# Gradient of a weight by Strassen pairs: one more pair, G's sums in one addition, PSUM banks filled ahead by ScalarE

## The chip, the cores and the metric

The kernel runs on one core of a Trainium2 chip. The metric is the device time of one execution in microseconds; a median over several runs is given. A core has a matrix engine (TensorE, in the profile PE for matmuls and PEld for loads of the stationary operand), a vector engine (VectorE, DVE), a scalar engine (ScalarE, ACT), GpSimd (POOL), which here only issues loads, and SyncE (SP), which issues stores. TensorE reads from SBUF and accumulates into PSUM; DVE and ACT move results from PSUM to SBUF.

## What is computed

```python
batch, m, k, n = 16, 512, 1024, 768
# input X: (16, 512, 1024) f32, grad_output G: (16, 512, 768) f32
grad_weight = np.einsum('bmk,bmn->kn', input, grad_output)   # (1024, 768) f32
```

With the batch and the rows taken together this is one product: the transpose of X (8192 x 1024) times G (8192 x 768), a sum over 8192 rows.

## The kernel before

The 8192 rows are taken in 32 units of 256 rows, two row tiles of 128 each. GpSimd's DMAs load a unit of X and of G and turn it from f32 to bf16 on the way. The output is cut into four quarters by X's columns (two halves of 512) and G's columns (two halves of 384): A and B are the left and right quarter of the upper half, C and D of the lower half. A quarter is four blocks of 128 x 384, one for each q, and each block takes one PSUM bank.

A unit is one of two kinds, by a letter of LOADS. For an "s" unit each of its two row tiles is multiplied plainly into A, B, C and D: 4 x 4 matmuls a tile, 32 a unit. A "P" unit is one step of Strassen's method on the 2 x 2 blocks that its two row tiles form: seven products in place of eight, each of four matmuls, 28 a unit, for the price of sums and differences of blocks that DVE makes first. Two of the seven products go to A and D directly; the other five (m, n, o, p, q) are gathered in `macc` and added to two quarters each at the end ("shares").

```python
LOADS = "sssssssPPPPPPPPPPPPPPPPPPPPPPPss"        # 9 single units, 23 pairs
...
def sum_g1(i):                                       # sums for pair i
    ge = sums.tile([P, 3, NH], bf16, name="ge")
    xe = sums.tile([P, 3, KH], bf16, name="xe")
    g = gp.rearrange("p m (h n) -> p m h n", h=2)
    nc.vector.tensor_add(out=ge[:, 0:2, :], in0=g[:, :, 0, :], in1=g[:, :, 1, :])     # L131
def sum_g2(i):
    nc.vector.tensor_add(out=extra[i][1][:, 2, :], in0=gp[:, 0, 0:NH], in1=gp[:, 1, NH:N])  # L135
def sum_g3(i):
    g = gp.rearrange("p m (h n) -> p (m h) n", h=2)
    nc.vector.tensor_sub(out=g[:, 1:3, :], in0=g[:, 1:3, :], in1=g[:, 3::-3, :])     # L140
def sum_x1(i): ...   # 1024 elements, L145
def sum_x2(i): ...   # 512 elements, L149
def sum_x3(i): ...   # 1024 elements, in place, L154
```

The order of all work is fixed by hand in a list of visits. `B14:2!0,2,0,0` means: visit product B, with its tiles up to the fourteenth; ACT takes the last two of its four banks and DVE the others; the exclamation mark closes the visit's banks, and the four numbers tell how many pieces of DVE work (sums for later pairs, shares) are put ahead of the drain of each bank. A number in front of the letter tells how many are put ahead of the visit. A visit that isn't closed stays open, and a later visit of the same product goes on in its banks. The eight banks form two slots of four, so two products are open at most.

```python
slots = [0, 1]
...
        if opening:
            slot = slots.pop(0)
            for q in range(Q):
                bank = psum.tile([P, 512], f32, name=f"bank{slot * Q + q}")[:, 0:NH]
                act = q >= Q - byact
                carried = act and not fresh[p]
                if carried:
                    nc.scalar.copy(out=bank, in_=sum_of(p, q))      # L266: ACT fills the bank with the sum so far
        ...
        nc.tensor.matmul(bank, stat, mov, start=..., stop=...)     # L285
        ...
        def shut(q):
            fill(ahead[q])
            if act:
                nc.scalar.copy(out=dst, in_=bank)                   # L299: ACT drains
            elif fresh[p]:
                nc.vector.tensor_copy(out=dst, in_=bank)            # L301
            else:
                nc.vector.tensor_add(out=dst, in0=bank, in1=dst)    # L303: DVE drains and adds
            if final and p in "ABCD":
                nc.sync.dma_start(out=OUT[...], in_=dst)
```

So a bank of ACT is first filled with the sum so far, which the matmuls then add to, and copied back at the end; a bank of DVE is added to the sum at the end. The last bank of the last visit is split into 256 and 128 columns (L336), with an addition and a store for each (L344). The very first tiles come as f32 over the queues of SP and ACT and are cast by DVE and ACT (`round_by`, L206), so that TensorE can start before GpSimd's first load lands; twelve matmuls of ones (L89) come before them.

Of the kernel before, what the change touches and what calls it, by code (L numbers as in the profile page):

```python
# [8 lines left out]

P = 128  # L10

LOADS = "sssssssPPPPPPPPPPPPPPPPPPPPPPPss"

ORDER = (
    "A1:3!0,0,0,0 D1:1 C2:4!0,0,0,0 B2:2!0,0,0,0 D3!0,0,0,0 A2 B4:1!0,0,0,0 A3 C4:2!0,0,0,0 "
    "A4!0,0,0,0 D5 D6!0,0,0,0 C6 B5 B6 B7 B8 C8!0,0,0,0 A8:1!0,0,0,0 D10:2!0,0,0,0 B10!0,0,0,0 "
    "A10:4 A12!0,0,0,0 C11!0,0,0,0 B14:2!0,2,0,0 C14:1!0,0,0,0 2D14:2 2A15:2!3,0,0,1 o2:4!2,0,0,0 "
    "m2:4!0,3,0,0 D15 n2:2!0,0,1,0 D16!0,0,0,0 q3:4!0,1,0,2 A16 p1:3 2p4!2,1,1,0 A18!2,0,0,0 m4:2 "  # L20
    "o5:4!2,2,0,0 m5!0,0,1,0 D19:1 4q6:4!2,0,0,0 D20!1,0,0,0 p5 p6 o7:1!1,0,0,0 n5:1 n7!5,0,0,0 "
    "p8 A20:4 3A22!3,0,1,0 p9!1,0,0,1 m9:3 D23:4!0,2,2,1 q10!1,0,1,0 m10 4o10:4 m11!0,1,0,0 "
    "o11!1,0,0,0 1n10 n11 2n12!2,0,0,0 p12:3!0,0,0,0 1A23 A24 1A25 1o13:3!3,0,0,2 A27!0,0,0,0 "
    "q12:3 D27:4 2q14!5,0,1,1 D28 1m15:2!2,0,0,2 p16:1!0,2,0,0 1D30!0,0,0,2 A30!0,0,0,0 o17:3 q16 "
    "8q18!0,0,0,1 o18 n16:4 4n19!0,2,0,3 D32 o20!1,0,1,1 D33 q20:2!1,0,0,0 D34!1,0,0,2 1m20:2 "
    "p17:4 m21!4,0,0,0 1p20 p22 3q22:2 3p23!2,0,0,0 q23!0,0,0,0 o23!0,0,0,0 A34:0-q m23:4!4,1,0,0 "
    "A37 n23:4!0,3,1,0 A41!1,0,1,0 C15:0+p C18!0,1,0,0 B18:4!0,0,1,2 D41!4,0,1,0 "
).split()


SHARES = (
    "t20 t21 t22 t23 t10 t11 t12 t13 l10 l11 l12 l13 l20 l21 l22 l23 l30 l31 l32 l33 "
).split()

WARMUP = [512] * 10 + [128] * 2
# [7 lines left out]
def kernel(  # L43
# [6 lines left out]
    nc = tc.nc  # L50
# [7 lines left out]
    NH = N // 2  # L58
    Q = KH // P

    X = input.rearrange("b m k -> (b m) k")
    G = grad_output.rearrange("b m n -> (b m) n")
    OUT = out.rearrange("(ks p) n -> p ks n", p=P)
# [14 lines left out]

    xf = [pairs.tile([P, K], f32, name=f"xf{s}", tag="xp") for s in range(2)]
    gf = pairs.tile([P, N], f32, name="gf", tag="gp")  # L80
    nc.sync.dma_start(out=gf[:, 0:NH], in_=G[0:P, 0:NH])  # L81
    nc.scalar.dma_start(out=xf[0], in_=X[0:P, :])
    nc.sync.dma_start(out=gf[:, NH:N], in_=G[0:P, NH:N])
    nc.scalar.dma_start(out=xf[1], in_=X[P : 2 * P, :])

    ones = nc.const_aps.tensor(1.0, (P, P), bf16)
# [38 lines left out]
    def sum_g1(i):  # L125
        _, xp, gp = items[i]
        ge = sums.tile([P, 3, NH], bf16, name="ge")
        xe = sums.tile([P, 3, KH], bf16, name="xe")
        extra[i] = (xe, ge)
        g = gp.rearrange("p m (h n) -> p m h n", h=2)  # L130
        nc.vector.tensor_add(out=ge[:, 0:2, :], in0=g[:, :, 0, :], in1=g[:, :, 1, :])  # L131

    def sum_g2(i):
        _, xp, gp = items[i]
        nc.vector.tensor_add(out=extra[i][1][:, 2, :], in0=gp[:, 0, 0:NH], in1=gp[:, 1, NH:N])  # L135

    def sum_g3(i):
        _, xp, gp = items[i]
        g = gp.rearrange("p m (h n) -> p (m h) n", h=2)
        nc.vector.tensor_sub(out=g[:, 1:3, :], in0=g[:, 1:3, :], in1=g[:, 3::-3, :])  # L140

    def sum_x1(i):
        _, xp, gp = items[i]
# [9 lines left out]
        x = xp.rearrange("p m (h k) -> p (m h) k", h=2)  # L153
        nc.vector.tensor_sub(out=x[:, 1:3, :], in0=x[:, 1:3, :], in1=x[:, 0::3, :])  # L154

    def settled(row, q):
        for p, (_, banks) in opened.items():
            assert p not in ("CD" if row else "AB") or not (banks[q][1] and banks[q][2])

# [10 lines left out]
    def share(name, q):  # L172
        left, right, row = SHARE_OF[name]
        sides = [
            (h, p)
            for h, p in enumerate((left, right))
            if p and ("ABCD"[(row > 0) * 2 + h], p) not in taken
        ]
        settled(row, q)
        if len(sides) == 2:  # L180
            a, b = SLOT[left], SLOT[right]
            dst = acc[:, row + q, :].rearrange("p (h n) -> p h n", h=2)
            src = macc[:, a : b + 1 : b - a, q, :]
        else:
            ((h, p),) = sides
            dst = acc[:, row + q, h * NH : (h + 1) * NH]
            src = macc[:, SLOT[p], q, :]
        op = nc.vector.tensor_sub if name[1] == "3" else nc.vector.tensor_add
        op(out=dst, in0=dst, in1=src)  # L189

    filler = []
    for i, item in enumerate(items):
        if item[0] == "P":
            filler += [(f, i) for f in (sum_g1, sum_g2, sum_g3, sum_x1, sum_x2, sum_x3)]
    filler += [(partial(share, c[:2]), int(c[2:])) for c in SHARES]
    filler.reverse()

# [8 lines left out]
        copy(out=dst[:, c0:c1], in_=src[:, c0:c1])  # L206

    x0, x1, g0 = items[0][1], items[1][1], items[0][2]
    round_by("DVE", g0, gf, 0, 192)
    round_by("ACT", g0, gf, 192, NH)  # L210
    round_by("DVE", x0, xf[0], 0, P)
    round_by("ACT", x0, xf[0], 2 * P, 4 * P)
    round_by("DVE", x0, xf[0], P, 2 * P)
# [9 lines left out]
    def operands(p, i, q):  # L223
        kind, x, g = items[i]
        k = slice(q * P, (q + 1) * P)
        k2 = slice(KH + q * P, KH + (q + 1) * P)
        left, right = slice(0, NH), slice(NH, N)
        if kind == "s":
            return x[:, k if p in "AB" else k2], g[:, left if p in "AC" else right]
        xe, ge = extra[i]  # L230
        return {
            "m": lambda: (xe[:, 2, k], ge[:, 2, :]),
            "n": lambda: (xe[:, 1, k], g[:, 0, left]),
            "o": lambda: (x[:, 0, k], g[:, 0, right]),
            "p": lambda: (x[:, 1, k2], g[:, 1, left]),
            "q": lambda: (xe[:, 0, k], g[:, 1, right]),
            "D": lambda: (x[:, 0, k2], ge[:, 0, :]),
            "A": lambda: (x[:, 1, k], ge[:, 1, :]),
        }[p]()

    def sum_of(p, q):
# [7 lines left out]
    slots = [0, 1]  # L249
    used = set()  # L250

    def visit(p, upto, byact, first, close, ahead, last):
        items_now = streams[p][done[p] : upto]
        done[p] = upto
        opening = p not in opened
        if opening:
            slot = slots.pop(0)
            banks = []
            for q in range(Q):
                name = f"bank{slot * Q + q}"  # L260
                bank = psum.tile([P, 512], f32, name=name)[:, 0:NH]
                act = q >= Q - byact
                carried = act and not fresh[p]
                if carried:
                    assert name in used
                    nc.scalar.copy(out=bank, in_=sum_of(p, q))  # L266
                elif first:
                    assert name in used and not fresh[p] and not byact
                    src = macc[:, SLOT[first[1]], q, :]
                    if first[0] == "-":  # L270
                        nc.scalar.mul(out=bank, in_=src, mul=-1.0)
                    else:
                        nc.scalar.copy(out=bank, in_=src)
                used.add(name)
                banks.append((bank, carried or bool(first), act))
            if first:
                taken.add((p, first[1]))
            opened[p] = (slot, banks)
# [3 lines left out]
        def mm(q, j):  # L282
# [8 lines left out]
                skip_group_check=carried,  # L291
            )

        def shut(q):
            fill(ahead[q])
            bank, _, act = banks[q]
            dst = sum_of(p, q)
            if act:
                nc.scalar.copy(out=dst, in_=bank)  # L299
# [3 lines that stand above are left out]
                nc.vector.tensor_add(out=dst, in0=bank, in1=dst)  # L303
            if final and p in "ABCD":
                row = q if p in "AB" else Q + q
                c0 = 0 if p in "AC" else NH
                nc.sync.dma_start(out=OUT[:, row, c0 : c0 + NH], in_=dst)

        if len(items_now) == 1:
            for q in range(Q):  # L310
# [4 lines left out]
        else:  # L315
# [10 lines left out]
            if q is not None:  # L326
# [1 line left out]
                fill(ahead[q])  # L328
                dst = sum_of(p, q)
                row = q if p in "AB" else Q + q  # L330
                b0 = 0 if p in "AC" else NH
                for c0, c1, name in ((0, 256, None), (256, NH, f"bank{slots[0] * Q}")):
                    bank = banks[q][0] if name is None else psum.tile([P, 512], f32, name=name)
                    for j in range(len(items_now)):
# [15 lines left out]
            slots.append(slot)  # L350

    rounded = False
    for n, step in enumerate(ORDER):
        step, _, ahead = step.partition("!")
        step, _, byact = step.partition(":")
        byact, first = byact[:1], byact[1:]
        at = next(c for c in step if c.isalpha())
        before, upto = step.split(at)
        if n == 1:
            round_by("DVE", g0, gf, NH, N)  # L360
        if not rounded and done[at] < 2 <= int(upto):
            rounded = True
            round_by("DVE", x1, xf[1], 4 * P, 6 * P)
            round_by("ACT", x1, xf[1], 6 * P, 8 * P)
            round_by("DVE", x1, xf[1], 0, 2 * P)
            round_by("ACT", x1, xf[1], 2 * P, 4 * P)
        fill(int(before or 0))
        ahead = [int(a) for a in ahead.split(",")] if ahead else None
        visit(at, int(upto), int(byact or 0), first, ahead is not None, ahead, n == len(ORDER) - 1)
    assert not filler and not opened  # L370


# [28 lines left out]
```

## Time and profile before

| what | value |
|---|---|
| time, median of 3 runs | 163.45 us (163.44 to 163.53) |
| span of the profiled execution | 161.9 us |
| granted TensorE clock | 1.00 |
| matmuls: warm-up, full width, split row | 12, 925, 14 |
| drains of PSUM banks by DVE / by ACT | 122 of 384 columns and the last two parts / 117 |
| fills of PSUM banks by ACT | 98 |
| HBM read | 58.72 MB |

The page gives busy time and share of the span for each engine, then the span in 40 equal slices with one digit each (9 is 90% or more). A busy PE is not PE at its peak: a matmul of 384 columns is listed with 326 ns, while consecutive ones start half that time apart. Pace is therefore read from start times. The chain of work that ended last is followed back from the last instruction; a timeline lists instructions in order of time, with start, duration, engine, line, operation and count, and in brackets the idle time before them and what ended it. A group line has count, busy time, mean ns of one, and idle time before.

### The profile page before, as it was taken

Reading aid. Unit: us, or ns where it says so; the run is one execution under the profiler, and the core shown is the slowest. Engines: PE = TensorE matmul, PEld = TensorE weight load, DVE = VectorE, ACT = ScalarE, POOL = GpSimd, SP = SyncE. Lnnn points to the kernel's source line nnn. Section 1 sums busy time; section 2 is a strip of 40 time slices with the busy share of each in tenths; the row PEclk is TensorE's granted clock in tenths of the full one; section 3 lists DMA queues with packets and bytes.
Section 4 is the critical chain, followed back from the end, with each engine's and each line's share of the span. In section 5 each row is a group of like instructions: output and inputs, shape, how many; then the busy total and the mean of one; then the engine's idle time right before and its main releaser. Section 6 shows DMA issues by size and latency. Waiting matters only on the chain.

```text
span 161.9 us, 2755 instructions
## 1 busy us (share of the span) xinstructions
PE 157.1 (97%) x951; PEld 92.7 (57%) x951; DVE 139.6 (86%) x289; ACT 94.6 (58%) x221; POOL 34.6 (21%) x69
## 2 busy tenths in 40 slices
PE   8799999999999999999999999999999999999992
PEld 2365666566565565655656666666555666666661
DVE  0557947469979999999989999999998999999992
ACT  3766004745587799359749684661446646888410
POOL 7442222122221212222212222222212100000000
PEclk9999999999999999999999999999999999999999
DMA  5999999999999999999999999999999999902675
GB/s 171 294 213 211 211 216 215 211 211 215 214 213 212 212 213 213 213 211 215 212 213 213 212 216 214 220 207 212 211 211 214 212 214 214 187 5 97 225 283 173
DMA packets 12397, 33.40 MB, mean 206 GB/s; under 512 B 1376, under 2 KB 4192, under 8 KB 12384
## 3 DMA queue, kind: packets, MB, share of 16 engines
q0 software_dynamic: 9360, 28.64, 89.4%
q1 hardware_dynamic: 2592, 3.47, 6.2%
q10 hardware_dynamic: 432, 1.11, 1.8%
q8 instruction: 7, 0.11, 0.3%
q14 instruction: 6, 0.05, 0.1%
HBM read 58.72 MB, written 3.15 MB: 382 GB/s over the span
## 4 chain that ended last, share of the span: by engine, by line
PE 93%; DMA 3%; DVE 1%; SPq 0%; issue 0%
PE bank L285 93%; DMA gf<-in_grad_output_dram 3%; PE bank L336 0%; DVE acc L344 0%; SPq L81 0%; DVE gp L206 0%
## 5 line engine op out<-in xcount | busy, mean ns | idle before, releaser
L285 PEld LDWEIGHTS <-xp 128*128 128x128 bf16 x649 | 63.3, 98 | 43.6 <-issue 1.5
L285 PE MATMUL bank<-gp,xp 128*128 128x384 bf16 x468 | 80.9, 326 | 1.0 <-DVE gp L206 1.0
L299 ACT COPY macc<-bank 128x384 f32<-128x384 f32 x73 | 31.5, 493 | 25.0 <-PE bank L285 24.9
L303 DVE TENSOR_TENSOR acc<-bank,acc 128x384 f32<-128x384 f32 x69 | 34.7, 551 | 8.7 <-PE bank L285 8.3
L285 PEld LDWEIGHTS <-xe 128*128 128x128 bf16 x276 | 26.6, 98 | 18.5 <-DVE xe L145 0.8
L285 PE MATMUL bank<-ge,xp 128*128 128x384 bf16 x181 | 33.6, 326 | 0.0
L285 PE MATMUL bank<-gp,xe 128*128 128x384 bf16 x184 | 32.4, 326 | 0.0
L266 ACT COPY bank<-macc 128x384 f32<-128x384 f32 x56 | 25.3, 503 | 8.0 <-DVE macc L303 6.9
L299 ACT COPY acc<-bank 128x384 f32<-128x384 f32 x44 | 19.5, 486 | 15.4 <-PE bank L285 15.3
L107 POOL DMA_DIRECT2D xp<-in_input_dram x30 | 15.9, 530 | 53.1 <-DMA xp<-in_input_dram 29.8
L106 POOL DMA_DIRECT2D gp<-in_grad_output_dram x30 | 15.9, 531 | 37.5 <-DMA gp<-in_grad_output_dram 14.8
L303 DVE TENSOR_TENSOR macc<-bank,macc 128x384 f32<-128x384 f32 x44 | 22.5, 552 | 1.5 <-PE bank L285 1.2
L266 ACT COPY bank<-acc 128x384 f32<-128x384 f32 x34 | 15.2, 492 | 8.6 <-DVE acc L303 8.5
L285 PE MATMUL bank<-ge,xe 128*128 128x384 bf16 x92 | 16.6, 326 | 0.0
L145 DVE TENSOR_TENSOR xe<-xp 128x1024 bf16<-128x1024 bf16 x23 | 15.7, 684 | 0.5 <-DMA xp<-in_input_dram 0.5
L154 DVE TENSOR_TENSOR xp<-xp 128x1024 bf16<-128x1024 bf16 x23 | 15.7, 684 | 0.0
L189 DVE TENSOR_TENSOR acc<-acc,macc 128x768 f32<-128x768 f32 (+1 forms) x20 | 14.6, 791 | 0.0
L131 DVE TENSOR_TENSOR ge<-gp 128x768 bf16<-128x768 bf16 x23 | 12.7, 551 | 0.2 <-DMA gp<-in_grad_output_dram 0.2
L140 DVE TENSOR_TENSOR gp<-gp 128x768 bf16<-128x768 bf16 x23 | 12.7, 551 | 0.0
L149 DVE TENSOR_TENSOR xe<-xp 128x512 bf16<-128x512 bf16 x23 | 9.6, 418 | 0.0
L135 DVE TENSOR_TENSOR ge<-gp 128x384 bf16<-128x384 bf16 x23 | 8.1, 351 | 0.0
L89 PE MATMUL bank<-const-bfloat16-1.0 128*128 128x512 bf16 (+1 forms) x12 | 4.6, 574 | 0.8 <-PEq L385 0.8
(20 smaller groups left out, 21.4 us busy)
## 6 DMA issues: line engine op xcount, KB each, us to landing
xp<-in_input_dram POOLq DMA_DIRECT2D x30, 512.0 KB, 16.7
gp<-in_grad_output_dram POOLq DMA_DIRECT2D x30, 384.0 KB, 16.7
out_dram<-acc SPq DMA_DIRECT2D x15, 192.0 KB, 1.9
xf<-in_input_dram ACTq DMA_DIRECT2D x2, 512.0 KB, 5.0
gp<-in_grad_output_dram POOLq DMA_DIRECT2D x3, 192.0 KB, 6.6
xp<-in_input_dram POOLq DMA_DIRECT2D x2, 256.0 KB, 7.9
gf<-in_grad_output_dram SPq DMA_DIRECT2D x2, 192.0 KB, 4.6
out_dram<-acc SPq DMA_DIRECT2D x1, 128.0 KB, 1.7
```

The source lines that it names most:

```text
L106: nc.gpsimd.dma_start(out=gp, in_=G[rows, :].rearrange("(p m) n -> p m n", m=2))
L107: nc.gpsimd.dma_start(out=xp, in_=X[rows, :].rearrange("(p m) k -> p m k", m=2))
L131: nc.vector.tensor_add(out=ge[:, 0:2, :], in0=g[:, :, 0, :], in1=g[:, :, 1, :])
L140: nc.vector.tensor_sub(out=g[:, 1:3, :], in0=g[:, 1:3, :], in1=g[:, 3::-3, :])
L145: nc.vector.tensor_add(out=xe[:, 0:2, :].rearrange("p a k -> p (a k)"), in0=xp[:, 0, :], in1=xp[:, 1, :])
L149: nc.vector.tensor_add(out=extra[i][0][:, 2, :], in0=xp[:, 0, 0:KH], in1=xp[:, 1, KH:K])
L154: nc.vector.tensor_sub(out=x[:, 1:3, :], in0=x[:, 1:3, :], in1=x[:, 0::3, :])
L189: op(out=dst, in0=dst, in1=src)
L266: nc.scalar.copy(out=bank, in_=sum_of(p, q))
L285: nc.tensor.matmul(bank, stat, mov, start=opening and j == 0 and not carried, stop=close and j == len(items_now) - 1, skip_group_check=car ...
L299: nc.scalar.copy(out=dst, in_=bank)
L303: nc.vector.tensor_add(out=dst, in0=bank, in1=dst)
```

## The change

A seventh single unit becomes the twenty-fourth pair, which takes four matmuls off the total. The three block sums of G are ordered so that they lie side by side and come out of one addition of 1152 elements, and the two differences are taken from the other two blocks; for this the names of the two column halves are exchanged (LEFT is now columns 384 to 767), and that half is loaded first. Where a visit is marked `~` or `^`, the fill of its banks by ACT is no longer issued when the visit opens, but behind the drains of the visit that leaves its slot: with `^` bank by bank behind each drain, with `~` behind the last. The order of the visits is new throughout (104 in place of 106, with 68 closings in place of 60).

```diff
-LOADS = "sssssssPPPPPPPPPPPPPPPPPPPPPPPss"
+LOADS = "ssssssPPPPPPPPPPPPPPPPPPPPPPPPss"
-    "A1:3!0,0,0,0 D1:1 C2:4!0,0,0,0 B2:2!0,0,0,0 D3!0,0,0,0 A2 B4:1!0,0,0,0 A3 C4:2!0,0,0,0 "
+    "A1:4!0,0,0,0 C1:3 B1:2 B2!0,0,0,0 C2!0,0,0,0 A2!0,0,0,0 D3:1 C3:2~ D4!0,0,0,0 C4!0,0,0,0 A4 "
...
+    "C9 A10:3^!0,0,0,0 C12!0,0,0,1 B12:1~!0,0,0,2 D12:1~ 2A12:4 A13!0,1,2,2 D13 p2:4!0,0,0,0 "
+    "n2:3!0,0,1,0 D14!0,0,0,0 m2:4!0,0,1,0 o3:4!3,0,0,0 1A15:1^!0,0,0,4 q3:4 q4!1,0,0,0 1p4:3~ "
...
+    "q24:2^!0,0,1,0 m24:3~!0,0,1,1 o24:3~!0,0,1,0 2n22:4~ 1n23 2A36:0-q n24!0,1,0,0 A39 "
+    "B16:4!0,3,1,0 2A40!0,0,0,0 C16:3!0,0,1,1 D40!0,1,1,0 "
...
+    LEFT, RIGHT = slice(NH, N), slice(0, NH)
-    nc.sync.dma_start(out=gf[:, 0:NH], in_=G[0:P, 0:NH])
+    nc.sync.dma_start(out=gf[:, LEFT], in_=G[0:P, LEFT])
...
-        g = gp.rearrange("p m (h n) -> p m h n", h=2)
-        nc.vector.tensor_add(out=ge[:, 0:2, :], in0=g[:, :, 0, :], in1=g[:, :, 1, :])
+        g = gp.rearrange("p m n -> p (m n)")
+        nc.vector.tensor_add(out=ge.rearrange("p a n -> p (a n)"), in0=g[:, 0 : 3 * NH], in1=g[:, NH : 4 * NH])
     def sum_g2(i):
-        nc.vector.tensor_add(out=extra[i][1][:, 2, :], in0=gp[:, 0, 0:NH], in1=gp[:, 1, NH:N])
-    def sum_g3(i):
         g = gp.rearrange("p m (h n) -> p (m h) n", h=2)
-        nc.vector.tensor_sub(out=g[:, 1:3, :], in0=g[:, 1:3, :], in1=g[:, 3::-3, :])
+        nc.vector.tensor_sub(out=g[:, 0::3, :], in0=g[:, 0::3, :], in1=g[:, 2:0:-1, :])
...
+    def carry(m, slot, q):
+        p, byact = steps[m][1], steps[m][3]
+        if q >= Q - byact:
+            bank = psum.tile([P, 512], f32, name=f"bank{slot * Q + q}")[:, 0:NH]
+            nc.scalar.copy(out=bank, in_=sum_of(p, q))
+            filled[m, q] = bank
...
                 if carried:
-                    nc.scalar.copy(out=bank, in_=sum_of(p, q))
+                    if not early:
+                        carry(n, slot, q)
+                    bank = filled.pop((n, q))
...
+            if follows is not None:
+                for b in ([q] if steps[follows][5] == "^" else range(Q) if q == Q - 1 else []):
+                    carry(follows, slot, b)
```

## The prediction

> **What bounds the kernel now.** I read the page first, then the chain that ended last, then the timelines of TensorE (PE), VectorE (DVE) and ScalarE (ACT), then the waits and the DMA landings. Busy shares and slices of the page:
>
> ```profile
> span 161.9 us, 2755 instructions
> ...
> PE 157.1 (97%) x951; PEld 92.7 (57%) x951; DVE 139.6 (86%) x289; ACT 94.6 (58%) x221; POOL 34.6 (21%) x69
> ...
> PE   8799999999999999999999999999999999999992
> ...
> DVE  0557947469979999999989999999998999999992
> ...
> DMA  5999999999999999999999999999999999902675
> ```
>
> PE is full from 7 us to the end, DVE nearly so from slice 11 on, and the DMA engines until about 141 us. The chain (start, us, what) says which of the three sets the end:
>
> ```profile
> 7.12 150.51 PE bank L285 x921
> ```
>
> It is one unbroken run of matmuls. The timeline of PE tells where that run starts and stops (start, duration, engine, line, operation, idle before):
>
> ```profile
> 5.21 0.96 PE L285 MATMUL bank<-gp,xp 128*128 128x384 bf16 x4
> 7.12 1.14 PE L285 MATMUL bank<-gp,xp 128*128 128x384 bf16 x6 [0.96 <-DVE gp L206]
> ...
> 157.48 0.49 PE L336 MATMUL bank<-ge,xp 128*128 128x256 bf16 x3
> ```
>
> The full-width (384-column) matmuls run from 7.12 to 157.48 us: 150.36 us for 921. In the trace consecutive starts lie 162 or 163 ns apart nearly everywhere, so 921 x 0.1625 = 149.66 us is pure pace, and only 0.70 us is waiting in the whole run. The last row is split into 256 and 128 columns; its pairs start every 109 + 56 = 165 ns, seven of them 1.16 us. PE is therefore done at 157.48 + 1.16 = 158.64 us, and 3.30 us of last additions and stores follow. So three things can shorten the run: fewer matmuls, the 0.96 us hole before 7.12, and the 0.70 us of waits. Nothing else counts unless it becomes a new wait.
>
> [...]
>
> ```profile
> L303 DVE TENSOR_TENSOR acc<-bank,acc 128x384 f32<-128x384 f32 x69 | 34.7, 551 | 8.7 <-PE bank L285 8.3
> ...
> L145 DVE TENSOR_TENSOR xe<-xp 128x1024 bf16<-128x1024 bf16 x23 | 15.7, 684 | 0.5 <-DMA xp<-in_input_dram 0.5
> ...
> L131 DVE TENSOR_TENSOR ge<-gp 128x768 bf16<-128x768 bf16 x23 | 12.7, 551 | 0.2 <-DMA gp<-in_grad_output_dram 0.2
> ...
> L135 DVE TENSOR_TENSOR ge<-gp 128x384 bf16<-128x384 bf16 x23 | 8.1, 351 | 0.0
> ```
>
> (551 - 351) / 384 = 0.52 ns per element[...]; the f32 drain of 384 costs as much as 768 bf16. [...]
>
> **The change, part by part.**
>
> (a) *One more pair.* A unit of 256 rows costs 2 x 16 = 32 matmuls as singles and 7 x 4 = 28 as a pair. Before: 9 x 32 + 23 x 28 = 932; after: 8 x 32 + 24 x 28 = 928. Four fewer: **-0.65 us**, all on the chain. One of them goes from the split row (last visit 6 tiles long, not 7).
>
> (b) *The order at the start.* Before, A1 is followed by D1, which needs the other half of G's first tile; that half lands at 6.69 us and its cast ends at 7.08, hence the hole. After, A1 is followed by C1, which uses the same half of G as A1 and the second half of X's tile; the three DVE casts of X run from 4.85 for 0.56 us and the two of ACT for 0.71, so X is there at 5.6. C1's four matmuls fit into the hole; B1, the first that needs the other half, starts at about 7.12. **-0.65 us.** The swap of the column halves (LEFT, RIGHT) itself moves no time: the half used first is still loaded first.
>
> (c) *One addition for G's three sums.* 1152 elements: 551 + 384 x 0.52 = 751 ns in place of 551 + 351 = 902. Instructions on DVE overlap by some 70 to 90 ns (in the timeline the sums start 470, 270, 470, 610, 340 and 600 ns apart, 2.76 us per pair), so the real gain is less: about 670 for 740, 2.69 us per pair. 24 x 2.69 - 23 x 2.76 = **+1.1 us of DVE**. The additions from PSUM fall from 113 to 110 full ones and the copies from 9 to 7 (5 x 0.47 = -2.4 us); the share additions become 16 x 0.87 + 4 x 0.47 in place of 12 and 8 (+1.6 us). DVE in sum: 139.6 to about 140 us, unchanged. None of it on the chain unless late.
>
> (d) *More, shorter visits, carried by ACT.* Drains rise from 60 x 4 to 68 x 4; ACT takes nearly all: its PSUM drains go from 117 to 154, its fills of banks from 98 to 129. 68 x 0.43 us (31.5 / 73) = +29 us, ACT from 94.6 to about 124 us, 77% of the span. Its fills are now issued right behind the drain of the same slot, before the ACT instructions of the visits between. I counted, for every opening of a bank, the matmuls that lie between its last one before and the next one: the least is 6 (0.98 us) both before and after, and with a fill 9 (1.46 us) both before and after; a drain (0.49) and a fill (0.50) fit. No new wait is certain here.
>
> (e) *Pairs begin one unit earlier.* The singles end after 192 matmuls, not 224. The loads stay as they are: in the trace a unit lands every 4.31 us (X of units 6, 7, 8, 9, 10, 11 at 34.36, 38.67, 43.89, 47.51, 51.83, 56.14). Before, DVE met exactly this:
>
> ```profile
> 43.91 0.69 DVE L145 TENSOR_TENSOR xe<-xp 128x1024 bf16<-128x1024 bf16 x1 [0.34 <-DMA xp<-in_input_dram]
> ```
>
> After, with matmul 8 at 7.12 us, the second tile of p2 (matmul 201, unit 7) is due at 7.12 + 193 x 0.1625 = 38.48, with earlier waits 38.6: 0.1 us of waiting. The third tile of o3 (matmul 230, unit 8) is due at 43.2, with the waits 43.45, and lands at 43.89: 0.45 us. Later needs (units 10, 11, 13, 15, 17) come 0.1 to 0.7 us after landing, and the lead grows by 28 x 0.1625 - 4.31 = 0.24 us a unit. For the singles (B2's casts on ACT behind four drains, A6 and C8 within 0.1 us of their landings) I take 0.15 us.
>
> *Sum.* Full-width matmuls after 7.12: 922 - 8 = 914 x 0.1625 = 148.53, so the split row starts at 155.65, takes 6 x 0.165 = 0.99, and ends at 156.64 + waits. Waits: 0.15 + 0.1 + 0.45 + 0.3 (for bank waits such as are in the 0.70 now; my choice) = 1.0. That is 157.64 against 158.64. The tail keeps its 3.30 us. 163.45 - 1.0 = **162.4 us**.
>
> **Rivals.**
>
> 1. *DVE becomes the bound.* For: from 60 to 150 us it is busy 88.25 of 90 us, and one late sum stops PE. To weigh it I added the start-to-start times of all DVE instructions behind one point (with 2% more, since the same sum over the whole kernel before gives 137.0 for its 139.6). After, from the X sum of unit 7 on, that is 116 us; from 38.67 it ends at 155, 2.6 us ahead of PE. Before, from the X sum of its second pair at 43.91, it was 113 us, ending at 157.3, 1.3 us ahead. So there is slightly more room than before. If short backlogs still hit PE, +1 us: 163.4.
> 2. *ACT's queue blocks.* [...] Against it: ACT would still be idle for 23% of the span. If twenty openings lose 0.1 us: +2 us, 164.5.
> 3. *The load is the bound early.* If unit 8 lands as late as 43.89 because of the traffic and units 7 and 9 too, the gains of (a) and (b) are waited away: 163.4. If instead unit 8 comes on the beat (43.0), 0.45 us is saved: 162.0.
> 4. *The tail.* Thirteen share additions in a row (11.3 us of DVE) come before the last drains; from the drain of o24 at about 139.9 they end at 151.2, A40's drains at 153.1, and the last bank is reached in step with PE. 1 us later at the start would show at the end.
>
> **Range and chances.** Best case waits 0.2 us: 161.6. A rival at work at half strength: 163.4. Range 161.6 to 163.4. Faster by over 2% means under 160.2 us, more than matmuls, hole and waits hold together (2.0 us): 0.01. Slower by over 2% is above 166.7, several rivals at once: 0.04.
>
> **What would show it.** 939 - 5 = 934 matmuls beside the warm-up; eight, not four, before 7.1 us; a hole of about 0.4 us there; the wide sum at about 750 ns; DVE about 140 and ACT about 124 us busy; PE waits on the X loads of units 7 and 8 near 38.6 and 43.5 us; the split row at about 156.6 us. Wrong would be: many gaps of PE behind ACT or DVE after 50 us, or the last additions standing long after PE's end.

## The result and the profile after

The changed kernel takes **164.62 us** (164.49 to 164.87, four executions) against 163.44 us for the kernel before: a ratio of 1.0073 [1.0055, 1.0090]. It is 1.2 us slower; 162.4 us was predicted, and the range ended at 163.4. Span, busy times, PE's slices and two groups of the page after:

```profile
span 163.0 us, 2787 instructions
...
PE 156.8 (96%) x946; PEld 92.0 (56%) x946; DVE 140.2 (86%) x266; ACT 122.0 (75%) x289; POOL 34.8 (21%) x69
...
PE   8899969999999999999999999999999999999992
...
L296 ACT COPY bank<-macc 128x384 f32<-128x384 f32 x64 | 29.4, 501 | 6.7 <-DVE macc L357 4.4
...
L138 DVE TENSOR_TENSOR ge<-gp 128x1152 bf16<-128x1152 bf16 x24 | 18.1, 753 | 0.0
```

Work is as expected: five matmul instructions fewer, DVE at 140 us, ACT at 122, the wide sum at 753 ns. The second slice of PE has risen from 7 to 8, so the start did get earlier. But the sixth slice, 20.4 to 24.5 us, has fallen from 9 to 6. The chain that ended last (start, duration, what) says who was waited for:

```profile
7.73 14.19 DMA xp<-in_input_dram
21.97 30.89 PE bank L337 x188
53.31 0.48 ACT macc L353
53.79 0.80 ACT bank L296 x2
54.59 1.17 ACT macc L353 x3
55.76 0.39 ACT bank L296
56.20 2.11 PE bank L337 x12
```

Before, one unbroken run of matmuls led from 7.12 us to the end. Now a load of X carries the chain until 21.97 us, and from 53 us on the chain leaves PE for short stretches of ACT and, further down, DVE. The timelines of PE from 15.5 to 23 us (start, duration, engine, line, shapes, count, idle before) show the first of these, in the kernel before and then after:

```profile
15.31 7.96 PE L285 MATMUL bank<-gp,xp 128*128 128x384 bf16 x48
```

```profile
15.32 5.28 PE L337 MATMUL bank<-gp,xp 128*128 128x384 bf16 x31
21.97 1.31 PE L337 MATMUL bank<-gp,xp 128*128 128x384 bf16 x7 [1.37 <-DMA xp<-in_input_dram]
```

Before has no break in these 8 us. After breaks at matmul 90 (counted from 0, without the warm-up), which is the third tile of the visit `C8:3~!` and the first use of X of unit 3. That load landed at 20.58 us in the profile before and at 21.92 after.

Taken from start times, with 162.5 ns for each full-width matmul, the two traces compare so:

| | before | after | difference |
|---|---|---|---|
| ninth matmul starts | 7.77 us | 6.49 us | -1.28 |
| full-width matmuls from there | 917, 149.01 us | 914, 148.53 us | -0.49 |
| waits among them | 0.69 us | 3.59 us | +2.90 |
| split row starts | 157.48 us | 158.61 us | +1.13 |
| from there to the end of the span | 4.46 us | 4.36 us | -0.10 |

The gains are there, 1.8 us of them, and 2.9 us of new waits take them away. (The two profiled executions differ by 1.03 us, the medians by 1.18.) Of the 3.59 us, **1.53** are at matmul 90; 0.54 are at matmuls 10 to 12, behind ACT's drains of A1 and a cast of X; 0.07 at matmul 64 on the load of unit 2; 0.94 behind fills and drains by ACT after 40 us, the longest 0.23; and 0.50 behind sums of DVE, the longest 0.25.

### The profile page after: what moved, and what is told of

Its sections match the earlier page's. It is cut to its first block, busy times and chain, and to the rows that moved or that the text cites. A ratio compares the mean times of both kernels' runs of the same rounds, so it can differ in the third digit from the quotient of the medians.

```text
span 163.0 us, 2787 instructions
## 1 busy us (share of the span) xinstructions
PE 156.8 (96%) x946; PEld 92.0 (56%) x946; DVE 140.2 (86%) x266; ACT 122.0 (75%) x289; POOL 34.8 (21%) x69
## 4 chain that ended last, share of the span: by engine, by line
PE 67%; DVE 14%; DMA 13%; ACT 2%; issue 2%; DVEq 0%; ACTq 0%; POOLq 0%
PE bank L337 66%; DMA xp<-in_input_dram 9%; DMA gp<-in_grad_output_dram 4%; DVE macc L357 3%; DVE ge L138 2%; DVE xe L148 2%; DVE gp L143 2%; DVE acc L357 2%; DVE xp L157 2%; ACT bank L296 1%; ACT macc L353 1%; DVE xe L152 1%; PE bank L392 0%; DVE acc L400 0%; DVEq L357 0%
## 5 line engine op out<-in xcount | busy, mean ns | idle before, releaser
L337 PEld LDWEIGHTS <-xp 128*128 128x128 bf16 x634 | 61.6, 98 | 44.9 <-DMA xp<-in_input_dram 2.0
L337 PE MATMUL bank<-gp,xp 128*128 128x384 bf16 x444 | 76.8, 326 | 2.1 <-DMA xp<-in_input_dram 1.4
L353 ACT COPY acc<-bank 128x384 f32<-128x384 f32 x71 | 31.1, 491 | 17.4 <-PE bank L337 17.0
L337 PEld LDWEIGHTS <-xe 128*128 128x128 bf16 x288 | 27.9, 98 | 19.5 <-DVE xe L148 0.5
L353 ACT COPY macc<-bank 128x384 f32<-128x384 f32 x83 | 35.4, 503 | 2.5 <-PE bank L337 2.4
L357 DVE TENSOR_TENSOR acc<-bank,acc 128x384 f32<-128x384 f32 x58 | 29.4, 552 | 9.0 <-PE bank L337 8.4
L296 ACT COPY bank<-macc 128x384 f32<-128x384 f32 x64 | 29.4, 501 | 6.7 <-DVE macc L357 4.4
L296 ACT COPY bank<-acc 128x384 f32<-128x384 f32 x61 | 27.5, 497 | 4.6 <-DVE acc L357 4.2
L357 DVE TENSOR_TENSOR macc<-bank,macc 128x384 f32<-128x384 f32 x52 | 26.5, 552 | 2.0 <-PE bank L337 2.0
L138 DVE TENSOR_TENSOR ge<-gp 128x1152 bf16<-128x1152 bf16 x24 | 18.1, 753 | 0.0
L194 DVE TENSOR_TENSOR acc<-acc,macc 128x768 f32<-128x768 f32 (+1 forms) x20 | 16.3, 873 | 0.0
```

Of the source, the lines that this page charges most:

```text
L138: nc.vector.tensor_add(out=ge.rearrange("p a n -> p (a n)"), in0=g[:, 0 : 3 * NH], in1=g[:, NH : 4 * NH])
L337: nc.tensor.matmul(bank, stat, mov, start=opening and j == 0 and not carried, stop=close and j == len(items_now) - 1, skip_group_check=car ...
```

## The experiments

Why did X of unit 3 land 1.3 us later in a kernel whose loads are the same? The DMA view by queue (packets, MB, share of 16 engines) from 19.5 to 20.4 us, first of after, then of before:

```profile
q0 software_dynamic: 69, 0.18, 102.6%
q8 instruction: 1, 0.02, 6.6%
```

```profile
q0 software_dynamic: 69, 0.18, 104.2%
```

After has a packet here that isn't a load: 16 KB on the queue of instructions, at 19.89 us, in the middle of X of unit 3. Before has its first such packet in the next slice of its trace, from 20.4 to 21.4 us:

```profile
q0 software_dynamic: 63, 0.19, 97.7%
q8 instruction: 1, 0.02, 5.9%
```

It starts there at 20.48 us, 0.10 us ahead of the landing of X of unit 3. The page after counts seven of them, 0.11 MB, so 16 KB each. From one to the next PE starts 232 to 274 matmuls and weight loads in the trace of after and 208 to 268 in that of before. The profile doesn't name the engine whose instructions they bring; that it is PE is the author's estimate from these counts.

**T1** was therefore: the instruction fetch takes time of a DMA engine from the load in flight, and PE's earlier start has moved it onto X of unit 3. The main rival, **T2**, was that the load of that unit is late by itself, by the order in which GpSimd issues it, fetch or no fetch. Either way the cure is to need the load later.

The traces also keep how a load lands. Each load signals its landing in sixteen steps, as many as the profile counts DMA engines (us, in order of time; run 2 is the second experiment below):

| load | issued | first step | fourteenth | fifteenth | sixteenth | first fetch |
|---|---|---|---|---|---|---|
| X of unit 3, before | 7.83 | 20.11 | 20.54 | 20.58 | 20.58 | 20.48 |
| X of unit 3, after | 7.73 | 20.00 | 20.47 | 20.48 | **21.92** | 19.89 |
| X of unit 3, run 2 | 7.71 | 19.93 | 20.42 | 20.46 | **21.80** | 19.72 |

After issues this load 0.10 us earlier than before does, and fifteen sixteenths of it are there 0.10 us earlier. One sixteenth alone is late, by 1.44 us. So the load as a whole does not come late, which speaks against T2; a single packet of 0.95 us on one engine is what T1 needs.

For the other waits: ACT's early fills (letter F in the expectations), the one wide sum of G (S) and relief of ACT's banks (B). All runs share a chip with runs of the kernel before, whose median was 163.49 to 163.57 us.

**1. A shorter warm-up in the kernel after, to move the fetch.**

```diff
-WARMUP = [512] * 10 + [128] * 2
+WARMUP = [512] * 8
```

> Changed kernel with a warm-up of 8 matmuls of 512 columns in place of 10 of 512 and 2 of 128: eight instructions fewer on TensorE ahead of the real work, nothing else. In the trace of the changed kernel a 16 KB transfer of the instruction queue starts at 19.89 us and the X tile of unit 3 lands at 21.92; in the kernel before it starts at 20.48 and the tile lands at 20.58. Theory T1 (the fetch of TensorE's instructions takes a DMA engine away from the load that is landing, and its time follows the count of TensorE's instructions): four matmul places later, 0.65 us, so the fetch starts at about 20.5, X of unit 3 lands at 20.5 to 20.6, the wait of 1.53 us at matmul 90 shrinks to about 0.1, and the time falls by 1.0 to 1.4 us, to 163.2 to 163.6. Rival T2 (the load itself is late, by the order in which GpSimd issues it): landing at 21.9 and 164.6 us as before. [...]

Measured: 164.60 us, ratio 1.0051 [1.0035, 1.0068], with a single one of 20 executions at 163.34. Its profile was taken at a granted clock of 0.95, so its times can't be compared closely with the others. In it the fetch starts at 19.91 us and X of unit 3 lands at 21.94: with eight instructions fewer the fetch is no later than the 19.89 of after. The execution at 163.34 was not profiled. So the load was not freed of the fetch, and this run doesn't decide between T1 and T2.

**2. A longer warm-up in the kernel before.** Nothing of the change is in it.

```diff
-WARMUP = [512] * 10 + [128] * 2
+WARMUP = [512] * 9 + [128] * 6
```

> Kernel before with a warm-up of 9 matmuls of 512 columns and 6 of 128 in place of 10 and 2: about as long (one of 512 for four of 128), with six instructions more. T1: the instruction fetch comes three matmul places earlier, at about 20.0 us in place of 20.48, falls on the X tile of unit 3, which lands at 21.8 or so; this kernel needs it at matmul 88, due at 20.83, so it waits about 1 us and the time rises from 163.44 to about 164.4. T2: the load is not touched, 163.4.

Measured: 164.73 us, ratio 1.0071 [1.0056, 1.0086]. The DMA view from 19.5 to 20.4 us and PE's timeline from 15.5 us of this run:

```profile
q0 software_dynamic: 66, 0.17, 95.3%
q8 instruction: 1, 0.02, 6.2%
```

```profile
15.33 5.38 PE L285 MATMUL bank<-gp,xp 128*128 128x384 bf16 x31
21.85 1.48 PE L285 MATMUL bank<-gp,xp 128*128 128x384 bf16 x8 [1.14 <-DMA xp<-in_input_dram]
```

The fetch came at 19.72 us, X of unit 3 landed at 21.80, and PE waits as in the kernel after. Three more warm-up matmuls, which compute nothing, cost the kernel before the same 1.2 us as the whole change. So the loss at matmul 90 needs neither the pair nor the new order. This is what T1 says, and T2 can't explain it.

**3. Needing unit 3 later, in the kernel after.** The visit of C is cut in two: its tiles of unit 2 come first for all four blocks, and only then those of unit 3. Six matmuls, 0.98 us, are thereby moved ahead of the first use of unit 3.

```diff
-C8:3~!0,0,0,0
+C6:3~ C8!0,0,0,0
```

> Changed kernel with the visit C8 (tiles 4 to 7 of each bank at once) taken as C6 and then C8: the two tiles of unit 2 for all four banks first, so that unit 3 is needed at matmul 96 in place of 90, 0.98 us later. No other change. If the late X tile of unit 3 is what costs (T1 and T2 alike), the wait of 1.53 us falls to about 0.55 and the time by 1.0 us to 163.6. If the 1.53 us would come back at a later wait anyway (the loads behind it being as late), 164.6.

Measured: 163.63 us, ratio 1.0006 [1.0000, 1.0013]. PE's timeline:

```profile
15.19 6.34 PE L337 MATMUL bank<-gp,xp 128*128 128x384 bf16 x37
21.98 1.31 PE L337 MATMUL bank<-gp,xp 128*128 128x384 bf16 x7 [0.44 <-DMA xp<-in_input_dram]
```

The fetch (19.85) and the landing (21.93) stay; six more matmuls run before the break, and the wait is 0.61 in place of 1.53 us. The kernel gains 1.0 us and stands level with the kernel before. So 0.92 us of this one wait make up most of the loss of 1.2.

**4. The two orders of casts exchanged**, so that the half of X that B1 needs is cast first.

```diff
+            round_by("DVE", x1, xf[1], 0, 2 * P)
+            round_by("ACT", x1, xf[1], 2 * P, 4 * P)
             round_by("DVE", x1, xf[1], 4 * P, 6 * P)
             round_by("ACT", x1, xf[1], 6 * P, 8 * P)
-            (the two lines of 0 to 4 * P stood here)
```

> Changed kernel with the casts of the second X tile in the order in which the new visits need them (the columns of B2 first, those of C2 after). B2 now starts at 7.67 us, on the cast that ends at 7.62. With the swap that cast ends at about 7.41; G's tile lands at 7.45, so B2 can start at 7.49. If nothing later takes it back: 0.2 us less, 164.4. But whatever is gained before matmul 90 is lost again where that waits for the load of unit 3 (T1 and T2): then 164.6, and the wait at matmul 90 grows by 0.2.

Measured: 164.58 us, ratio 1.0061 [1.0045, 1.0078]. B2 starts at 7.45 in place of 7.67 us, but the gain doesn't even reach matmul 90. Matmul 64, the first on unit 2, waits 0.25 us in place of 0.07 for X of unit 2, which lands at 16.10 us, and starts at 16.14 in place of 16.20. The wait at matmul 90 is then 1.45 us (fetch 19.76, landing 21.79); it did not grow by 0.2. What is saved before a load is worth nothing while that load sets the time, and unit 2 is as close a bound as unit 3.

**5. Without early fills.** All `~` and `^` are taken out, so each fill is issued when its visit opens.

```diff
-    "B4:2~ A6!0,0,0,0 ... D8:1^!0,0,0,0 ..."
+    "B4:2 A6!0,0,0,0 ... D8:1!0,0,0,0 ..."
```

> Changed kernel with every mark for the early fills taken away: ACT fills a visit's banks when the visit opens, behind the ACT instructions of the visits between, as the kernel before does. Same matmuls, same drains, same order of visits. In the changed kernel the waits of TensorE that end with an ACT fill are 0.9 us in sum (from 54 us on). Theory F1 (the early fill puts a copy that must wait for a drain at the head of ACT's queue and holds back others): these waits fall, 0.3 to 0.6 us less, 164.1. Theory F2 (the new order with its 129 fills needs the early fills): they rise to 2 us or more, 165.5 or above.

Measured: 177.33 us, ratio 1.0829 [1.0779, 1.0878]. The waits of PE (us in total, times, longest) say why:

```profile
PE bank L337 <- ACT bank L296: 9.6, 13, 1.3
PE bank L337 <- DMA xp<-in_input_dram: 1.2, 1, 1.2
```

Thirteen waits on fills, up to 1.3 us each, stand where after has waits of at most 0.23. F2 was right, with 9.6 us where it had named 2 or more. In this order, with its 68 closings, the early fills are worth 13 us; they don't cause the loss.

**6. G's three sums in two additions**, of 768 and 384 elements, everything else as after.

```diff
-        nc.vector.tensor_add(out=ge.rearrange(...), in0=g[:, 0 : 3 * NH], in1=g[:, NH : 4 * NH])
+        (the same in two additions, of the first 2 * NH and the last NH elements)
```

> Changed kernel with the three block sums of G made by two additions of 768 and 384 elements in place of one of 1152; all else the same. By the start-to-start times this adds 0.07 us of DVE per pair, 1.7 us in all. Theory S1 (DVE is what the chain goes through from 77 to 102 us, and it is late there): the wait at matmul 578, 0.25 us, grows by about 0.4 (six pairs by 0.07), time 165.0. Theory S2 (DVE has room): no change, 164.6, and then the single addition is worth nothing.

Measured: 165.11 us, ratio 1.0080 [1.0060, 1.0101]. The groups of the two additions:

```profile
L139 DVE TENSOR_TENSOR ge<-gp 128x768 bf16<-128x768 bf16 x24 | 13.2, 549 | 0.0
L140 DVE TENSOR_TENSOR ge<-gp 128x384 bf16<-128x384 bf16 x24 | 8.4, 349 | 0.0
```

898 ns in place of 753, and the waits behind DVE's sums grow: 0.30, 0.07 and 0.37 us at matmuls 445, 554 and 578, where after has 0.09, none and 0.25. The wide sum saves about 0.5 us of the whole, as S1 says. It too is not the cause.

**7. A much longer warm-up in the kernel after**, to move the fetch ahead of unit 3.

```diff
-WARMUP = [512] * 10 + [128] * 2
+WARMUP = [128] * 42
```

> Changed kernel with a warm-up of 42 matmuls of 128 columns, about as long as that of 10 of 512 and 2 of 128 but with 60 instructions more. T1 (the fetch follows TensorE's count of instructions and delays the loads in flight): it comes 30 matmul places, 4.9 us, earlier, at about 15.0 us, so now X of unit 2 lands late (16.16 before, some 17 now), the wait moves from matmul 90 to matmul 64 (unit 2, 0.9 to 1.3 us there, and less than 0.6 at 90); the time stays within 0.5 of 164.6. T2 (X of unit 3 is late by itself): unit 2 lands at 16.1 and unit 3 at 21.9 as now, 164.6.

Measured: 164.67 us, ratio 1.0041 [1.0018, 1.0063]. Its executions lie in two groups, 163.8 to 164.2 and 164.6 to 164.9 us; the profile is one of the first group. (Runs 8, 9 and 10 have two such groups as well, 0.4 to 1.1 us apart, so their medians depend on how many executions fall in each. Two of the twenty of run 6 lie 1.1 us below the rest, and 13 of the 153 of the kernel before at 165.0 to 165.2 us, 0.9 us or more above all its others; none of these was profiled.) There the fetch came at 15.68 us. It was expected to hit X of unit 2; it hit G of unit 3 (18.73 us, where runs 2 and 3 have 18.0), and X of unit 3 landed at 21.16:

```profile
21.21 1.96 PE L337 MATMUL bank<-gp,xp 128*128 128x384 bf16 x11 [0.68 <-DMA xp<-in_input_dram]
```

The wait is half as long (0.84 us from start times). The load that was hit is not the one foretold, but again it is one at the moment of the fetch, here the next in the queue.

**8. Runs 3, 4 and 1 together**: unit 3 later, casts exchanged, eight warm-up matmuls.

> Changed kernel with three edits: unit 3 needed at matmul 96 (C6, then C8), the casts in the order of need, and the warm-up of 8 matmuls, eight instructions fewer. Where the fetch falls behind the X tile of unit 3 (20.5 to 20.6 us), matmul 96 can start at 20.8 to 21.0 and the time is 162.5 to 162.8, below the kernel before; where it falls on that tile, matmul 96 starts at 21.98 whatever comes before, and the time is 163.6 as with the first edit alone. By the run with the shorter warm-up, where one execution in twenty was at 163.34 and the others at 164.6, T1 makes two separate values likely rather than one between; T2 gives 163.6 always.

Measured: 163.78 us, ratio 1.0017 [0.9994, 1.0039]. The profile (164.36 us, of the upper group) shows the opposite case to after. DMA view from 20.4 to 21.4 us, and PE's timeline:

```profile
q0 software_dynamic: 63, 0.19, 97.7%
q8 instruction: 1, 0.02, 5.9%
```

```profile
15.30 7.96 PE L337 MATMUL bank<-gp,xp 128*128 128x384 bf16 x48
```

The fetch came at 20.86 us, behind X of unit 3, all of which was there at 20.61. So where the fetch falls behind the load, the load is on time. From matmul 60 to 200 there is no wait at all, but this doesn't show what the earlier landing is worth: the first twelve matmuls here start about 320 ns apart, twice the usual distance, so PE comes to matmul 96 only at 22.6 us and would not have waited for a landing at 21.9 either.

**9. Run 8 with the warm-up of run 7.**

> Changed kernel with unit 3 needed at matmul 96, the casts in the order of need, and the warm-up of 42 matmuls of 128 columns. With that warm-up the fetch came at 15.7 us, delayed G of unit 3 (18.73 for 18.0), and X of unit 3 landed at 21.16. Matmul 96 is then due at about 21.0 to 21.1 and waits 0.1 us or less, where it waited 0.6 with the landing at 21.93. T1: 163.0 to 163.2 us, below the 163.5 of the kernel before, for executions with the early fetch; where the fetch is later, 163.6. T2 (landing late by itself): 163.6.

Measured: 164.53 us, ratio 1.0038 [1.0017, 1.0058]. The lower group, 163.26 to 163.60 us, is no faster than the kernel before either. PE's timeline, from the upper group (164.77 us):

```profile
15.20 1.14 PE L337 MATMUL bank<-gp,xp 128*128 128x384 bf16 x6
17.81 5.37 PE L337 MATMUL bank<-gp,xp 128*128 128x384 bf16 x32 [1.48 <-DMA xp<-in_input_dram]
```

The fetch came at 15.73 us and this time hit X of unit 2, which landed at 17.77 in place of about 16.15 us.

**10. Run 9 with one bank of ACT given to DVE in each of two visits**, those whose fills PE waited for near 56 and 58 us.

```diff
-1p4:3~  ...  D17:2!0,0,0,1
+1p4:2~  ...  D17:1!0,0,0,1
```

> The kernel of the run before this with two bank jobs moved from ACT to DVE around 50 to 57 us: the visit p4 gives ACT two banks in place of three, the visit D17 one in place of two. That takes two fills and two drains (1.7 us) off ACT and puts two additions (0.94 us) on DVE. Theory B1 (the waits at matmuls 298 and 310, 0.22 and 0.20 us, are ACT's queue: three drains of p and then the fills of D and o stand one behind the other): both fall below 0.05 us, time 0.3 to 0.4 us lower. Rival B2 (DVE is the nearer bound there): waits on DVE sums of the same size take their place and the time stays or rises.

Measured: 164.18 us, ratio 1.0065 [1.0042, 1.0088]. The two waits on ACT (0.23 and 0.20 us) are gone, and PE's waits of this run name what came instead:

```profile
PE bank L337 <- DVE gp L143: 0.4, 1, 0.4
PE bank L337 <- DVE xp L157: 0.3, 1, 0.3
```

By start times these are 0.57 and 0.49 us, 1.06 in place of 0.43. In DVE's timeline the sums of units 10 and 11 stand behind the added drains. The lower median is no gain: by groups, run 10 has 163.96 to 164.21 and 165.29 to 165.57 us where run 9 has 163.26 to 163.60 and 164.42 to 165.14, about 0.6 us less, and seven of twelve executions in the lower group where run 9 has eight of 22. So B2 was right: this edit moved the waits to DVE and made them longer.

**11. Runs 3 and 4 with the usual warm-up.**

> The kernel of the first run of this set with the warm-up of the kernel before (10 of 512, 2 of 128). Only the warm-up differs. T1: the fetch comes at 19.7 to 19.9 us, X of unit 3 lands at 21.8 to 21.9, matmul 96 waits about 0.7 us, 163.6: the 0.2 us of the swapped casts are lost in that wait. T2: the same as with the other warm-up.

Measured: 163.59 us, ratio 0.9997 [0.9981, 1.0013]; fetch 19.87, X of unit 3 21.95, a wait of 0.59 us at matmul 96. The only edit between this and run 9 is the warm-up, and X of unit 2 is on time again (16.15 us): it was the moved fetch that had delayed it.

**12. Run 11 with nine warm-up matmuls of 512.**

> The changed kernel with C6 before C8 and the casts in the order of need, and a warm-up of 9 matmuls of 512 columns: six instructions fewer than with the usual warm-up, 0.4 us of warm-up less. T1: the fetch comes three matmul places, 0.5 us, later, at about 20.35 us, close behind the last of X of unit 3; where it misses that tile, this lands at 20.5 to 20.6, matmul 96 starts at 21.2 without a wait, and the time is 162.9 to 163.1, below the kernel before; where it still falls on it, 163.6. [...] T2: 163.6 always.

Measured: 163.65 us, ratio 1.0001 [0.9984, 1.0018]. The fetch was to move behind the load; it came at 19.70 us, earlier than in run 11 (19.87). X of unit 3 landed at 21.74, and the wait was 0.31 us. Six instructions fewer of PE did not delay the fetch.

Eight profiles, ordered by the first fetch:

| kernel | first fetch, us | load that was hit, us | X of unit 3, us |
|---|---|---|---|
| run 7 | 15.68 | G of unit 3, 18.73 | 21.16 |
| run 9 | 15.73 | X of unit 2, 17.77 | 21.45 |
| run 12 | 19.70 | X of unit 3 | 21.74 |
| run 2 (order before) | 19.72 | X of unit 3 | 21.80 |
| run 11 | 19.87 | X of unit 3 | 21.95 |
| after | 19.89 | X of unit 3 | 21.92 |
| before | 20.48 | G of unit 4, 23.27 | 20.58 |
| run 8 | 20.86 | G of unit 4, 23.07 | 20.61 |

The others fit in: fetches at 19.76 to 19.91 us with landings at 21.79 to 21.94 (runs 1 and 3 to 6), and for run 10 15.87 with 21.36. In the load that the table gives as hit, the last step comes 0.6 to 1.6 us behind the fifteenth; in the load just before it, at most 0.12 us. There is no version that beats the kernel before by more than the uncertainty; runs 3, 11 and 12 equal it.

## Why the prediction was wrong

**The step that failed** is the sentence "The loads stay as they are", and with it the term "For the singles ... I take 0.15 us". The term assumed that A6 and C8 come within 0.1 us of their landings in the trace before. C8's third tile waited 1.53 us, A6 0.07 and matmuls 10 to 12 another 0.54: 2.14 us for the 0.15. The landing times of the kernel before were not a property of its loads: the instruction fetch happened to fall at 20.48 us, just as X of unit 3 was done, and an earlier PE brought it forward. Run 2 against the kernel before, and runs 8 and 9 against run 11, show by the warm-up alone that the landings change. Even with the landing of 20.58 us, matmul 90, due at 6.49 + 0.54 + 0.07 + 82 x 0.1625 = 20.43 us, would have waited 0.15 us (an estimate from the trace): a start earlier than that has no room left to earn in.

Point by point:

(a) Right: 934 matmuls, three full-width ones and one pair of the split row fewer. 0.49 us of it is in the table, the rest behind the start of the split row. The prediction's three things that can shorten the run take the pace for fixed; both traces keep it (97% of the full-width starts before and 95% after come 162 or 163 ns behind the one ahead), but that no change could shorten it was not shown.

(b) Right in direction, too small: the ninth matmul starts at 6.49 us, not 7.12. The surplus belongs to the profile before rather than to the change: G's other half landed at 6.69 us there, at 5.98 after. In run 2, with the order of before and three more warm-up matmuls, the ninth is at 7.08, so the change itself brings 0.59 us. But then B1 and B2 wait 0.54 us, for which, together with A6 and C8, the prediction had 0.15.

(c) Right: 753 ns against 751, DVE 140.2 against "about 140". Run 6 adds that the narrower form would cost 0.5 us.

(d) "No new wait is certain here" and 0.3 us for bank waits: too small. It was 0.94 us behind ACT and 0.50 behind DVE. The busy time was right (122 against 124 us), and so was the room of one drain and one fill. What failed was counting each bank for itself: in the chain above, the third bank of the visit D17, which PE starts at 56.20 us, stands behind three drains of the visit p5, whose banks it takes over, and then its own fill, 1.56 us of ACT in a row (54.59 to 56.15), more than the room for one of each. The two longest of these waits are in D17 and o6, neither of which is marked for an early fill; whether a mark there would help was not tried. This is rival 2 in a mild form, less than half of its 2 us. A fill that waits for DVE does hold back the next drain: in the trace of after ACT stands idle for 1.99 us until the fill of 90.78 us, which waits for an addition to `acc`, and the drain behind it starts at 91.20, 2.6 us after the start of the last matmul into its bank (matmul 495, 88.58 us). Rival 1 came true at about half its size, and run 10 shows one trade between the two engines that loses.

(e) The 0.55 us at units 7 and 8 did not occur. PE came to matmul 230 only at 44.88 us, not 43.45, and X of unit 8 landed at 42.87, not 43.89. The 43.89 of the trace before, from which the prediction took its largest single wait, bears the same sign of a fetch: there the second fetch starts at 41.80 us, fifteen steps of X of unit 8 are in by 42.98, on the beat of 4.31 us, and the sixteenth is 0.91 us late. After has its second fetch at 43.66 us, behind this load. So rival 3 named the right mechanism, a load that waits the early gains away, with the wrong unit and without its cause.

The tail was right: 3.43 us from the last matmul's start, before 3.36. Rival 4 did not appear.

By its own sum the split row was to start at 156.65 us; it started at 158.61, 1.96 us later: 0.63 less from the start, 2.59 more from waits (3.59 against 1.0), of which 1.53 are at matmul 90.

What stays open: what exactly sets the moment of the fetch. Adding 6 or 60 PE instructions brought it forward (runs 2 and 7), taking 6 or 8 away did not put it back (runs 12 and 1), and the one late fetch (run 8) went along with a slow start. Counted in the traces, PE has started 197 to 199 matmuls and weight loads when the first fetch begins in all kernels with 12 or 15 warm-up matmuls, 185 to 191 with eight or nine, and 209 with 42. So the fetch keeps close to PE's place in its program, and a PE that gets there earlier brings it forward, as T1 took it, but the count isn't constant, and runs 1, 8 and 12 relied on its being so. It was not found out whether the 1.5 us of bank and sum waits after 40 us would show in full if the early break were gone; run 8, the only profile of the new order without a wait on unit 2 or 3, had lost its time at the start. Nor was a run profiled in the lower group of runs 8 and 9.

## What to carry to other kernels

Here the loads keep the DMA engines busy at nine tenths or more (the page's slices 2 to 34), and the first uses come within a few tenths of a microsecond of the landings. A landing time was then no fixed input of the estimate: in run 2, three more warm-up matmuls brought the first fetch from 20.48 to 19.72 us and moved the landing of X of unit 3 from 20.58 to 21.80. Look for such fetches in the DMA view of the stage before counting on a landing; and before counting a gain at the start, ask where the next load binds, and put some work in front of that first use, as run 3 did for 1.0 us.

## What was not expected of the hardware

A fetch of 16 KB, listed with about 0.95 us, made one sixteenth of a load of 512 KB land 1.3 to 1.4 us after the rest and so, in a kernel bound by that load, cost 1.2 us of 163 (run 2). In both kernels one sixteenth stayed 0.81 to 0.89 us behind in every load from G of unit 4 to X of unit 6; on both pages the DMA engines are busy at nine tenths or more in all slices of that time, which by the author's reading left hardly a pause to catch up in. Before lost this time on G of unit 4 (23.27 us), where nobody waited. And the first real matmuls start at 320 ns from start to start in place of 162 in some profiles: about twelve of them in run 8, with a warm-up of eight matmuls of 512, and two or three in runs 9 and 10, with 42 of 128. In the profile of run 1, with the same eight, they start 163 to 174 ns apart, so the warm-up's length alone does not decide it.
